# RWKV branch of a hybrid decoder trunk: eight heads in one chain, each head of a pair on its own partition half

## Chip, cores and metric

The kernel runs on one core of a Trainium2 chip. The metric is the device time of one execution in microseconds; a kernel's time is the median of its runs.

## Reference

A trunk of two layers works on 256 tokens of width 1024 in fp32. Each layer adds three branches (RWKV, a short convolution, attention with a forget gate), each behind a sigmoid gate and an up-projection, then `w_out`, a layer norm, a feed-forward part and a second layer norm. The feed-forward part is dense in the first layer, and two of eight experts per token in the second. The change concerns the RWKV branch, with eight heads of 64 channels:

```python
p = p + mu_shift * (token_shift(p) - p)
r, k, v, w_lo, a_lo, g_lo = _split_cols(p, ...)
decay = jnp.exp(-jnp.exp(-jax.nn.softplus(-w_raw) - 0.5))   # w_raw = w0_decay + tanh(w_lo) @ w2_decay
a = jax.nn.sigmoid(a0 + a_lo @ w2_iclr)
g = jax.nn.sigmoid(g_lo) @ w2_gate
kk = _heads(k * k_k); kk = kk / jnp.maximum(jnp.linalg.norm(kk, axis=-1, keepdims=True), 1e-12)
k = k * (1.0 + (a - 1.0) * k_a)
# for each token t and head, a_t = -kk, b_t = kk * a:
state = state * d_t + (state @ a_t) b_t^T + v_t k_t^T ;  y_t = state @ r_t
# then: norm of y per head, times lnx_g plus lnx_b, plus sum(r * k * r_k) * v, times g
```

## The kernel before

The kernel holds activations with channels on partitions and the 256 tokens along the columns, as a tile `[128, j, 256]` for each two heads per 128 channels. The weights of all projections are streamed from HBM on SP's queue in tiles of 1 MB (`st`, three buffers). ScalarE rounds each tile to a high half (`hi`, line 94) and VectorE makes the rest (`lo`, line 97). A product is then three passes of the rounded kind (fp32r): `hi` by `hi`, `hi` by `lo`, `lo` by `hi`. One helper issues them all, and so all carry line 116. The small products of the RWKV branch are ordinary fp32 matmuls with lines of their own.

A scheduler fixes the order of each engine's instructions when the kernel is compiled, and prefers what comes first in the program among what it holds to be ready. So PE's queue in a mixer is a mix: blocks of small RWKV matmuls, and between them runs of projection passes (line 116) of whatever projection comes next.

In a mixer (`mixer_body`) the order of the program is: the projection of the lora inputs (`lo_in`, line 349); the two groups' decay, in-context rate and gate (`lora_group`, line 370, whose matmuls are line 364); then `rwkv_group` twice, for heads 0 to 3 and for heads 4 to 7; then the forget attention (lines 603 to 697), the convolution, the three up-projections. `open_next` (line 700) opens the next stage, and its loads are on SP. What a group does:

- Project k, r and v (`lerp_pair`, line 395: a projection and the token shift), and scale k by its norm. `rs_expand` (line 329) sums squares by head, takes an inverse root, transposes it, and spreads it over the head's channels by a matmul with a constant of four rows (line 344).
- Make `ar` and `bk` (lines 407 to 413), for each chunk of 64 tokens a pair of 64 columns, and from them the score matrix `MT` (line 429), 128 by 128 for each head and chunk: sixteen in a group. A head of a pair has its channels on partitions 0 to 63, the other on 64 to 127.
- Invert the unit triangular 64 by 64 part of each of the sixteen matrices. The diagonal blocks of 16 are inverted by VectorE, a column at a time (lines 447 to 450), all sixteen at once on 64 partitions; then blocks of 32 and of 64 are put together by matmuls, in two halves `q` of eight matrices (lines 472, 477, 481) and one piece of sixteen (line 487). `B` and `BT` (lines 454 to 465) hold the inverse and its transpose.
- Transpose v and `bk` on PE: v by a multiplication with the identity into partitions 64 to 127 (line 498), `bk` by transposes (line 505).
- Run the chain over four chunks (lines 511 to 551). `X` is the state's part (line 515, a state of two heads as a 128 by 128 tile with zeros off the diagonal blocks) plus v's part (line 517); `U` is the inverse by `X` (line 524); the state's update is line 529; the output is the state's part (line 545) plus that of U and v (line 548). ScalarE copies X and U, VectorE updates the state `S`, and GpSimd clears it first (line 532).
- Norm, gain, bonus and gate of y (lines 553 to 567), written to `oh` and `ol` as two halves.

The chain's central lines:

```python
nc.tensor.matmul(pX[:, j, :], ar[:, 4 * j + c, 0, :], Sp[:, j, :], start=True, stop=False)
nc.tensor.matmul(pX[:, j, 64 * h:64 * h + 64], MT[64:128, j, h, c, 0, :], UV[64:128, c, j, h, :], ...)
nc.tensor.matmul(pU[:, j, h, :], TT[:, j, h, c, :], X[:, j, h, :], start=True, stop=True)
nc.tensor.matmul(pD[:, j, :], BKt[:, c, j, :], UV[:, c, j].rearrange("p h v -> p (h v)"), start=True, stop=True)
```

Of the kernel before, what the change touches and what calls it, by code (L numbers as in the profile page):

```python
# [12 lines left out]
F32 = mybir.dt.float32  # L13
F32R = mybir.dt.float32r
# [23 lines left out]
K_ID, K_BO, K_MK, K_M1, K_RST, K_BS, K_EX, K_CM, K_TRI, K_IOTA, NCONST = (  # L38
    0, 128, 256, 384, 448, 704, 706, 962, 1346, 1474, 1602)
# [11 lines left out]
def tile_kernel(ctx, tc, x_in, wmix, wf_in, cols_in, bfor_in, lora_in, lnrow_in, wffn, rw_in, rb_in, wmoe,  # L51
# [202 lines left out]
    LATE = {"cst", "cols", "hcols", "lora", "merged", "raw", "dd", "k", "r", "v", "oh0", "ol0", "oh1", "ol1", "upad", "yv"}  # L254
# [6 lines left out]
    def mixer_body(l, xTh, xTl, mp, lp, es, open_next):  # L261
# [22 lines left out]
        mask1 = cst[0:64, K_M1 - P:K_M1 - 64]  # L284
        bsel = cst[0:64, K_BS - P:K_BS + 2 - P]
        expd = cst[0:4, K_EX - P:K_EX + P]
# [17 lines left out]
        lerp_n = [0]  # L304

        def lerp_pair(key, dst_tag, bufs):
# [6 lines left out]
            o = mt([P, 2, T], dst_tag, bufs=bufs)  # L313
            for j in range(2):
                nc.vector.scalar_tensor_tensor(o[:, j, :], dd[:, j, :], col(C_MU + lerp_n[0]),
                                               raw[:, j, 1:T + 1], ALU.mult, ALU.add)
                lerp_n[0] += 1
            return o

        merged = mt([P, KD, T], "merged")  # L320
# [8 lines left out]
        def rs_expand(sq, scale, eps, op):  # L329
            pc = psC()  # L330
            for tc_ in range(2):
                for j in range(2):
                    nc.tensor.matmul(pc[:, 4 * tc_ + 2 * j:4 * tc_ + 2 * j + 2], sq[:, j, tc_ * P:(tc_ + 1) * P],
                                     bones[:, 0:P:64], start=True, stop=True)
            r8 = sm.tile([P, 8], F32, tag="r8", name=nm("r8"))
            rsqrt_small(r8, pc[:, 0:8], 8, scale, eps, op)
            pt = psC()
            for tc_ in range(2):
                nc.tensor.transpose(pt[0:4, tc_ * P:(tc_ + 1) * P], r8[:, 4 * tc_:4 * tc_ + 4], ident)
# [3 lines left out]
            for j in range(2):  # L343
# [3 lines left out]
        W3 = [P, 2, T]  # L347
        NU = 8
        lo_in = lerp_pair("lo", "lo_in", 1)
# [4 lines left out]
        def lora_mm(g, kind):  # L354
            pz = psC().rearrange("p (j t) -> p j t", j=2)
            for j in range(2):
                ct = 2 * g + j
                if kind == 0:
                    a, b = lora[0:64, ct * P:(ct + 1) * P], lo_in[0:64, 0, :]
                elif kind == 1:  # L360
                    a, b = lora[64:128, ct * P:(ct + 1) * P], lo_in[64:128, 0, :]
                else:
                    a, b = lora[:, 512 + ct * P:512 + (ct + 1) * P], lo_in[:, 1, :]
                nc.tensor.matmul(pz[:, j, :], a, b, start=True, stop=True)
            return pz

        f2 = lambda t: t.rearrange("p j t -> p (j t)")
        u3 = lambda t: t.rearrange("p j (c s) -> p (j c) s", s=64)

        def lora_group(g):  # L370
            sg = mt(W3, "sg")
            tanh2(sg, lora_mm(g, 0), C_W0 + 2 * g)
            half_up(sg)
            cs = mt(W3, "cs")
            for j in range(2):
                nc.vector.tensor_tensor_scan(cs[:, j, :], rst, sg[:, j, :], 0.0, ALU.mult, ALU.add)
            pdec = mt([P, NU, 65], f"pdec{g}")
            nc.gpsimd.memset(pdec[:, :, 0:1], 1.0)
            nc.scalar.activation(pdec[:, :, 1:65], u3(cs), AF.Exp, scale=-DECAY_C)
# [942 lines left out]
```

## Time and profile before

| | us |
|---|---|
| median of 3 runs | 1951.13 |
| lowest and highest run | 1950.76, 1959.35 |
| span of the profiled execution | 1953.1 |
| PE busy in it | 1897.4 |
| VectorE busy | 1529.9 |
| ScalarE busy | 1143.3 |

The profile is one execution, whose span of 1953.1 us stands beside the median of 1951.13. In it the first layer's mixer runs from 16.6 us to some 340, the dense feed-forward part to 553, the second layer's mixer from 570 to some 905, and the experts from 947 to the end. Engines are PE (TensorE), DVE (VectorE), ACT (ScalarE), POOL (GpSimd) and SP; a q behind one is its DMA queue. In rows of PE `a*b` is the stationary operand's shape and `a x b` the result's; `xN` counts passes, of which an ordinary fp32 matmul makes two, and an fp32r matmul or a transpose one. The granted clock is given as a share of 2.4 GHz.

### The profile page before, as it was taken

To read this page: it belongs to the slowest core of one execution; us is meant where nothing else is said; L and a number is where in the kernel's file an instruction comes from. 1 tells how busy PE (TensorE), PEld (TensorE's weight loads), DVE (VectorE), ACT (ScalarE), POOL (GpSimd) and SP (SyncE) were. 2 spreads that over 40 slices of the span, in tenths; PEclk is the share of its full clock that TensorE was granted. 3 is DMA by queue.
4 is the path that set the end of the run, shared out by engine and by line. 5 is a ranking of instruction groups with operands and counts; after the bars stand their busy time and mean duration, and the time that the engine had idled before them with its cause. 6 is when DMAs were issued, how large, how long until landed. Compare 5 with 4: busy or idle time off the path is not lost.

```text
span 1953.1 us, 29168 instructions
## 1 busy us (share of the span) xinstructions
PE 1897.4 (97%) x11285; PEld 1641.8 (84%) x11285; DVE 1529.9 (78%) x2153; ACT 1143.3 (59%) x1460; POOL 40.6 (2%) x94
## 2 busy tenths in 40 slices
PE   7999999999999999999799999999999999999997
PEld 6888899899878888998688888888888888888885
DVE  7958366755569566566899999999899998998987
ACT  5344245344434444344577777777777777777774
POOL 0010000000000010000200000000000000000000
PEclk9999899999999798999799999999999999999998
DMA  7313165555543122486499998999999999899980
GB/s 263 130 46 110 63 216 176 209 180 185 189 166 130 66 87 88 145 328 265 183 377 369 352 370 325 369 370 349 366 333 364 370 355 368 330 356 375 357 314 24
DMA packets 69730, 489.09 MB, mean 250 GB/s; under 512 B 8528, under 2 KB 8784, under 8 KB 11344
## 3 DMA queue, kind: packets, MB, share of 16 engines
q1 hardware_dynamic: 69008, 485.05, 66.9%
q8 instruction: 90, 1.47, 0.3%
q10 hardware_dynamic: 576, 2.10, 0.3%
q14 instruction: 56, 0.46, 0.1%
HBM read 483.98 MB, written 3.15 MB: 249 GB/s over the span
## 4 chain that ended last, share of the span: by engine, by line
PE 59%; DVE 2%; issue 0%; ACT 0%; DVEq 0%
PE A L116 20%; PE B L116 17%; PE C L116 17%; PE Y L977 1%; PE D L977 1%; DVE x L249 0%; PE A L932 0%; PE Y L116 0%; PE D L116 0%; DVE x L242 0%; PE B L932 0%; DVE lo L97 0%; PE Y L1019 0%; PE Y L1018 0%; PE D L1019 0%; PE D L1018 0%
## 5 line engine op out<-in xcount | busy, mean ns | idle before, releaser
L97 DVE TENSOR_TENSOR lo<-st,hi 128x1024 fp32r<-128x1024 f32 x892 | 1050.3, 1220 | 190.8 <-ACT hi L94 156.2
L94 ACT CAST hi<-st 128x1024 fp32r<-128x1024 f32 x896 | 895.8, 1049 | 428.8 <-PE A L116 194.1
L116 PE MATMUL C<-hi,hT 128*128 128x512 f32 x880 | 224.5, 396 | 0.0
L116 PE MATMUL A<-xTh,hi 128*128 128x256 f32 x1280 | 200.8, 296 | 0.0
L116 PEld LDWEIGHTS C<-hi,hT 128*128 128x128 f32 x880 | 164.7, 188 | 37.4 <-ACT hT L979 0.2
L116 PE MATMUL A<-xTl,hi 128*128 128x256 f32 x1280 | 193.3, 290 | 0.0
L116 PE MATMUL A<-xTh,lo 128*128 128x256 f32 x1280 | 191.8, 290 | 0.0
L116 PE MATMUL A<-hi,xTh 128*128 128x512 f32 x448 | 180.7, 403 | 0.0
L116 PEld LDWEIGHTS A<-xTh,hi 128*128 128x128 f32 x1280 | 174.4, 198 | 6.1 <-issue 3.1
L116 PE MATMUL A<-lo,xTh 128*128 128x512 f32 x448 | 175.5, 392 | 0.4 <-DVE lo L97 0.4
L116 PE MATMUL B<-hi,xTh 128*128 128x512 f32 x448 | 175.4, 391 | 0.0
L116 PE MATMUL B<-lo,xTh 128*128 128x512 f32 x448 | 175.1, 391 | 0.0
L116 PE MATMUL A<-hi,xTl 128*128 128x512 f32 x448 | 174.8, 390 | 0.0
L116 PE MATMUL B<-hi,xTl 128*128 128x512 f32 x448 | 174.6, 390 | 0.0
L116 PEld LDWEIGHTS A<-xTl,hi 128*128 128x128 f32 x1280 | 171.3, 196 | 2.9 <-issue 1.1
L116 PEld LDWEIGHTS A<-xTh,lo 128*128 128x128 f32 x1280 | 170.9, 196 | 1.6 <-issue 0.3
L116 PE MATMUL C<-lo,hT 128*128 128x512 f32 x440 | 120.3, 395 | 0.0
L116 PEld LDWEIGHTS A<-lo,xTh 128*128 128x128 f32 x448 | 84.1, 188 | 20.4 <-DVE lo L97 2.4
L116 PEld LDWEIGHTS C<-lo,hT 128*128 128x128 f32 x440 | 83.1, 189 | 19.7
L116 PEld LDWEIGHTS A<-hi,xTl 128*128 128x128 f32 x448 | 84.1, 188 | 18.3
L116 PEld LDWEIGHTS B<-hi,xTl 128*128 128x128 f32 x448 | 84.1, 188 | 18.1
L116 PEld LDWEIGHTS B<-lo,xTh 128*128 128x128 f32 x448 | 84.1, 188 | 17.7 <-issue 0.2
(478 smaller groups left out, 2100.3 us busy)
## 6 DMA issues: line engine op xcount, KB each, us to landing
st<-in_wmoe_dram SPq DMA_DIRECT2D x336, 1024.0 KB, 6.9
st<-in_wmix_dram SPq DMA_DIRECT2D x82, 1024.0 KB, 4.9
st<-in_wffn_dram SPq DMA_DIRECT2D x33, 1024.0 KB, 4.9
xsc<-x ACTq DMA_DIRECT2D x4, 512.0 KB, 4.6
x<-xsc SPq DMA_DIRECT2D x4, 512.0 KB, 5.6
g<-in_lnrow_dram SPq DMA_DIRECT2D x2, 1024.0 KB, 6.5
st<-in_lnrow_dram SPq DMA_DIRECT2D x2, 1024.0 KB, 8.3
cst<-in_const_dram SPq DMA_DIRECT2D x2, 609.0 KB, 11.0
```

Source lines behind the costliest of these rows:

```text
L94: nc.scalar.copy(hi, st[:, h * 1024:(h + 1) * 1024])
L97: (eng or nc.vector).tensor_tensor(lo, st[:, h * 1024:(h + 1) * 1024], hi.bitcast(F32), ALU.subtract)
L116: last = nc.tensor.matmul(o, a, b, start=start and i == 0, stop=stop and i == 2)
L977: nc.tensor.transpose(pt[:, i * P:(i + 1) * P], h[:, i * P:(i + 1) * P], ident)
```

## The change

`rwkv_group` and `lora_group` are gone; their steps stand once, for all eight heads.

- Order: k of both groups, then the norms for all eight heads, then r of both, then v of both. The weight tiles are loaded in the order k0, k1, r0, r1, v0, v1 (before: k0, r0, v0, k1, r1, v1).
- `rs_expand` works on four pairs of heads. The inverse root is split into two halves of the rounded kind in one tile `rT` of 40 rows (rows 0 to 7 and 32 to 39, zeros between), and spread by one fp32r matmul for each pair of heads; its constant `exps` (40 by 512) is a DMA of its own and is cast by ScalarE.
- `bk` holds its two parts in opposite order for the two heads of a pair, so that the head on partitions 0 to 63 and the one on 64 to 127 each have all that belongs to them on their own half. The inverse runs on 128 partitions, both heads of a pair side by side; its matmuls and those of the chain alternate between the two heads, each in its own quarter or half of the array.
- v is transposed by PE transposes ahead of the chain, and its part of X, `XV`, is made ahead of the chain for all chunks; in the chain VectorE adds it to the state's part.
- The state is 64 columns for each pair of heads in place of 128 with zeros, so GpSimd's clears are gone; the last columns of the decay are kept in `PL`. U and the inverse's last copies are shared by ScalarE and VectorE.
- Buffers are shared anew: `MT` takes the place of the lora outputs (`W16`), `UV` of `pdec` and `kx` (`U8`), the transposed `bk` is written in place; the attention's `qk` and `oct_` lie in `merged`'s tile, the first gates' tiles in those of k and r.

```diff
+                for j in range(4):
+                    nc.tensor.matmul(pc[:, 8 * tc_ + 2 * j:8 * tc_ + 2 * j + 2], sq[:, j, tc_ * P:(tc_ + 1) * P],
...
-            rT = mt([4, T], "lo_in")
-            nc.vector.tensor_copy(rT, pt[0:4, 0:T])
-            pe = psC().rearrange("p (j t) -> p j t", j=2)
-            for j in range(2):
-                nc.tensor.matmul(pe[:, j, :], expd[:, j * P:(j + 1) * P], rT, start=True, stop=True)
-            return pe
...
+                nc.tensor.transpose(pt[0:8, tc_ * P:(tc_ + 1) * P], r16[:, 8 * tc_:8 * tc_ + 8], ident)
+            nc.scalar.copy(rT[0:8], pt[0:8, 0:T])
+            nc.vector.tensor_tensor(rT[32:40], pt[0:8, 0:T], rT[0:8].bitcast(F32), ALU.subtract)
...
+            for g in range(2):
+                pe = psC().rearrange("p (j t) -> p j t", j=2)
+                for j in range(2):
+                    nc.tensor.matmul(pe[:, j, :], expdr[:, (2 * g + j) * P:(2 * g + j + 1) * P], rT,
+                                     start=True, stop=True)
+                out.append(pe)
...
+        exps = mt([40, 512], "N1")
+        nc.sync.dma_start(exps, const_in[0:40, NCONST:NCONST + 512])
+        expdr = mt([40, 512], "expdr", F32R)
+        nc.scalar.copy(expdr, exps)
+        rT = mt([40, T], "rT", F32R)
+        nc.vector.memset(rT.bitcast(F32), 0.0)
...
+        k4, r4, v4 = mt(W4, "k"), mt(W4, "r"), mt(W4, "v")
+        for g in range(2):
+            lerp_pair(f"k{g}", k4[:, 2 * g:2 * g + 2], 2 + 6 * g)
...
+        for h in range(2):
+            r = HALF[h]
+            nc.vector.tensor_tensor(bk[r, :, h, :], u4(kx)[r], u4(pinv)[r], ALU.mult)
+            nc.vector.tensor_tensor(bk[r, :, 1 - h, :], u4(k2)[r], u4(pinv)[r], ALU.mult)
...
+        MT = mt([P, 4096], "W16").rearrange("p (h j c a t) -> p h j c a t", h=2, j=4, c=4, a=2)
+        for j in range(4):
+            pS = [psC(), psC()] if j % 2 == 0 else [psD(), psY()]
+            for c in range(4):
+                u = 4 * j + c
+                for h in range(2):
+                    r = HALF[h]
+                    nc.tensor.matmul(pS[h][:, c * P:(c + 1) * P], bk[r, u].rearrange("p a s -> p (a s)"),
+                                     ar[r, u].rearrange("p a s -> p (a s)"), start=True, stop=True)
...
+        dd_ = mt([P, 16, 32], "dblk")
+        for h, hf, r, q in quads:
+            nc.vector.transpose(dd_[r].rearrange("p t s -> p (t s)"),
+                                MTu[h][r, :, 0, q].rearrange("p u (w t) -> p t w u", w=2))
...
+        for t in range(1, 16):
+            nc.vector.tensor_tensor(tmp[:, 0:t, 0:t], tt[:, 0:t, 0:t],
+                                    dg[:, t, 0:t].unsqueeze(1).to_broadcast([P, t, t]), ALU.mult)
+            nc.vector.tensor_reduce(tt[:, 0:t, t], tmp[:, 0:t, 0:t], mybir.AxisListType.X, ALU.add)
...
+        B = mt([P, 16, 64], "B")
+        nc.vector.transpose(flat(B), flat(TT))
...
+        pW = psC().rearrange("p (u s) -> p u s", u=16)
+        for u in range(16):
+            for r in HALF:
+                nc.tensor.matmul(pW[r, u, :].rearrange("p (w r) -> p w r", w=2), N1[r, u, :], Bf[r, u],
+                                 start=True, stop=True)
+        nc.scalar.copy(W1, pW)
+        pX = psC().rearrange("p (u s) -> p u s", u=16)
+        for u in range(16):
+            for r in HALF:
+                nc.tensor.matmul(pX[r, u, :], TT[r, u, :], W1[r, u, :], start=True, stop=True)
+        nc.vector.tensor_tensor(Bf, pX.rearrange("p u (w r) -> p u w r", w=2), Bf, ALU.add)
+        nc.vector.transpose(flat(TT), flat(B))
+        pW = psC().rearrange("p (u s) -> p u s", u=16)
+        up_, dn = [slice(0, 32), slice(64, 96)], [slice(32, 64), slice(96, 128)]
+        for u in range(16):
+            for h in range(2):
+                nc.tensor.matmul(pW[dn[h], u, :], MTu[h][up_[h], u, 0, 32:64], B[up_[h], u, 0:32], start=True, stop=True)
...
+        pX = psC().rearrange("p (u s) -> p u s", u=16)
+        for u in range(16):
+            for h in range(2):
+                nc.tensor.matmul(pX[up_[h], u, :], W2[dn[h], u, :], TT[dn[h], u, 32:64], start=True, stop=True)
...
+        for cc in range(2):
+            pv = psD() if cc else psY()
+            for j in range(4):
+                nc.tensor.transpose(pv[:, j * P:(j + 1) * P], v4[:, j, cc * P:(cc + 1) * P], ident)
...
+        XV = mt([P, 4, 4, 64], "B")
+        for cp in range(2):
+            px = psC().rearrange("p (c j v) -> p c j v", c=2, j=4)
+            for ci in range(2):
+                c = 2 * cp + ci
+                for j in range(4):
+                    for h in range(2):
+                        k_ = HALF[1 - h]
+                        nc.tensor.matmul(px[HALF[h], ci, j, :], MT[k_, h, j, c, 0, :], UV[k_, c, h, j, :],
+                                         start=True, stop=True)
+            nc.scalar.copy(XV[:, 2 * cp:2 * cp + 2], px)
+        for j in range(4):
+            pk = psC()
+            for c in range(4):
+                nc.tensor.transpose(pk[:, c * P:(c + 1) * P], bk[:, 4 * j + c].rearrange("p a s -> p (a s)"), ident)
+            nc.scalar.copy(bk[:, 4 * j:4 * j + 4].rearrange("p c a s -> p c (a s)"), pk.rearrange("p (c n) -> p c n", c=4))
...
+        Sp = None
+        for c in range(4):
+            if c:
+                pX = psC()[:, 0:256].rearrange("p (j v) -> p j v", j=4)
+                for j in range(4):
+                    for r in HALF:
+                        nc.tensor.matmul(pX[r, j, :], ar[r, 4 * j + c, 0, :], Sp[r, j, :], start=True, stop=True)
+                X = mt([P, 4, 64], "dg")
+                nc.vector.tensor_tensor(X, pX, XV[:, c], ALU.add)
+            else:
+                X = XV[:, 0]
+            pU = psC()[:, 0:256].rearrange("p (j v) -> p j v", j=4)
+            for j in range(4):
+                for r in HALF:
+                    nc.tensor.matmul(pU[r, j, :], TT[r, 4 * j + c, :], X[r, j, :], start=True, stop=True)
+            for h, eng in enumerate((nc.scalar.copy, nc.vector.tensor_copy)):
+                eng(UV[HALF[h], c, h], pU[HALF[h]])
+            if c < 3:
+                pD = psD()[:, 0:256].rearrange("p (j v) -> p j v", j=4)
+                for j in range(4):
+                    for h in range(2):
+                        nc.tensor.matmul(pD[HALF[h], j, :], bk[:, 4 * j + c, h, :], UV[:, c, h, j, :],
+                                         start=True, stop=True)
+                Sn = mt([P, 4, 64], "S", bufs=2)
+                pl = PLj[:, :, c:c + 1].to_broadcast([P, 4, 64])
+                if c:
+                    nc.vector.tensor_tensor(Sn, pD, Sp, ALU.add)
+                    nc.vector.tensor_tensor(Sn, Sn, pl, ALU.mult)
+                else:
+                    nc.vector.tensor_tensor(Sn, pD, pl, ALU.mult)
+            py = psY()[:, 0:256].rearrange("p (j t) -> p j t", j=4)
+            if c:
+                for j in range(4):
+                    for r in HALF:
+                        nc.tensor.matmul(py[r, j, :], Sp[r, j, :], ar[r, 4 * j + c, 1, :], start=j == 0, stop=False,
...
+            for j in range(4):
+                for h in range(2):
+                    nc.tensor.matmul(py[HALF[h], j, :], UV[:, c, h, j, :], MT[:, h, j, c, 1, :],
+                                     start=c == 0 and j == 0, stop=True, skip_group_check=True)
+            nc.scalar.copy(y[:, :, 64 * c:64 * c + 64], py)
+            if c < 3:
...
+        oct_ = big[:, 1024:2048].rearrange("p (c n) -> p c n", c=2)
+        gk, gr = mt(W4, "k"), mt(W4, "r")
...
-                qk = mt([72, 2, T], "qk", bufs=2)
+                qk = big[0:72, 512 * h:512 * h + 512].rearrange("p (j t) -> p j t", j=2)
...
```

## Rows read from the trace of the kernel before

**Rows 1.** The page's busy times by engine (its part 1: busy us, share of the span, instructions), and the chain that ended last, its share of the span by engine (part 4).

```profile
PE 1897.4 (97%) x11285; PEld 1641.8 (84%) x11285; DVE 1529.9 (78%) x2153; ACT 1143.3 (59%) x1460; POOL 40.6 (2%) x94
...
PE 59%; DVE 2%; issue 0%; ACT 0%; DVEq 0%
```

**Rows 2.** The view by windows, two stretches of the first layer's mixer: RWKV's whole work, and what follows it up to 345 us. Columns: the window, its length, then busy us (instructions) of PE, PEld, DVE, ACT and POOL, the granted clock of PE as a share of 2.4 GHz, the DMA share and GB/s.

```profile
16.58:258.53 241.95, 236.88 (x1877) 210.97 (x1877) 167.04 (x400) 104.36 (x188) 11.37 (x36) 0.95 0.31 109
258.53:345.00 86.47, 86.47 (x720) 86.20 (x719) 57.66 (x75) 42.96 (x55) 0.44 (x5) 1.00 0.60 209
```

**Rows 3.** The chain of waits in order of time, 800 to 890 us: a run of projections in the second layer's mixer, nothing else between them. Columns: start, length in us, engine, tile, line, instructions.

```profile
821.58 40.31 PE A L116 x336
```

**Rows 4.** The timeline of PE, 218 to 243 us: the chain over chunks in the first layer, with runs of projections between its blocks. Columns: start and length in us, engine, line, operation, out<-in, the sizes, the passes. Lengths overlap at the ends.

```profile
222.23 0.45 PE L548 MATMUL Y<-MT,UV 128*64 128x64 f32 x8
222.62 0.74 PE L116 MATMUL A<-xTl,hi 128*128 128x256 f32 x4
...
230.39 0.43 PE L515 MATMUL D<-S,ar 128*64 128x128 f32 x2
230.75 0.44 PE L517 MATMUL D<-UV,MT 64*64 64x64 f32 x4
231.12 0.43 PE L515 MATMUL D<-S,ar 128*64 128x128 f32 x2
231.49 0.44 PE L517 MATMUL D<-UV,MT 64*64 64x64 f32 x4
231.86 0.74 PE L116 MATMUL A<-xTl,hi 128*128 128x256 f32 x4
232.53 0.67 PE L524 MATMUL D<-X,BT 64*64 64x64 f32 x8
233.13 1.22 PE L116 MATMUL A<-xTh,lo 128*128 128x256 f32 x8
234.19 0.60 PE L529 MATMUL D<-UV,BKt 128*128 128x128 f32 x4
234.72 0.34 PE L548 MATMUL Y<-MT,UV 128*64 128x64 f32 x4
234.99 0.43 PE L545 MATMUL Y<-ar,S 128*128 128x64 f32 x2
235.35 0.34 PE L548 MATMUL Y<-MT,UV 128*64 128x64 f32 x4
235.62 0.73 PE L116 MATMUL B<-oh,hi 128*128 128x256 f32 x4
```

**Rows 5.** The timeline of PE, 24 to 37 us and 60 to 100 us, and last the costliest lines of PE, 0 to 400 us, for line 429 (busy us, mean ns of one | idle time before them and what ended it).

```profile
26.99 1.14 PE L364 MATMUL C<-lo_in,lora 64*128 64x256 f32 x8
28.06 0.39 PE L116 MATMUL A<-xTh,hi 128*128 128x256 f32 x1
...
62.58 1.16 PE L429 MATMUL C<-ar,bk 64*128 64x128 f32 x8
63.66 0.50 PE L116 MATMUL A<-xTl,hi 128*128 128x256 f32 x2
...
L429 PE MATMUL C<-ar,bk 64*128 64x128 f32 x64 | 8.1, 285 | 0.2 <-DVE MT L432 0.2
```

**Rows 6.** The timeline of PE, 100 to 150 us: the solve's matmuls and the transposes of the first group.

```profile
102.98 1.11 PE L472 MATMUL C<-B,N 64*64 64x32 f32 x16
104.03 0.73 PE L116 MATMUL A<-xTl,hi 128*128 128x256 f32 x4
...
108.74 1.19 PE L487 MATMUL C<-BT,dblk 32*32 32x32 f32 x32
109.86 1.09 PE L498 MATMUL C<-ident,v 128*64 128x128 f32 x8
110.88 0.43 PE L681 MATMUL B<-lora,pT 128*128 128x64 f32 x2
...
112.13 0.60 PE L505 MATMUL C<-ident,bk 128*128 128x128 f32 x4
112.66 1.09 PE L498 MATMUL C<-ident,v 128*64 128x128 f32 x8
```

**Rows 7.** The costliest lines of PE, 0 to 400 us, for line 344 (busy us, mean ns of one | idle time before them).

```profile
L344 PE MATMUL C<-lo_in,cst 4*128 4x256 f32 x16 | 4.5, 400 | 0.0
```

**Rows 8.** The waits of PE, 16 to 262 us: the tile and line that waited, who released it, then the total us, the number of waits and the longest.

```profile
PE C L472 <- DVE B L465: 2.4, 2, 1.4
```

**Rows 9.** The view by windows, the four stretches around the solves, two in each layer (columns as in rows 2).

```profile
93.00:114.00 21.00, 20.45 (x209) 18.39 (x210) 8.67 (x25) 9.70 (x22) 1.47 (x4) 0.84 0.29 101
194.00:218.00 24.00, 23.63 (x199) 21.48 (x200) 7.99 (x12) 5.41 (x9) 0.00 (x0) 0.64 0.26 88
646.00:677.00 31.00, 30.76 (x221) 27.85 (x221) 10.35 (x27) 10.20 (x22) 1.47 (x4) 0.56 0.20 68
755.00:769.00 14.00, 13.46 (x104) 12.45 (x104) 6.45 (x9) 2.69 (x6) 0.00 (x0) 0.63 0.28 82
```

**Rows 10.** The view by windows from the first projection to the first solve (columns as in rows 2), and the costliest lines of VectorE in the same stretch, for line 97.

```profile
16.58:93.00 76.42, 73.75 (x517) 66.21 (x516) 68.88 (x138) 37.75 (x53) 4.52 (x19) 1.00 0.46 164
...
L97 DVE TENSOR_TENSOR lo<-st,hi 128x1024 fp32r<-128x1024 f32 x23 | 27.7, 1212 | 0.0
```

**Rows 11.** The timeline of SP's queue: start and length of two issues of DMAs behind the first layer's RWKV work.

```profile
259.66 0.81 SPq L748 DMA_DIRECT2D x<-xsc  x2
```

More of the change, by code (lines that the diff above doesn't have):

```diff
@@ new lines, in mixer_body @@
+        k2 = cs
+        for j in range(4):
+            nc.vector.tensor_scalar(k2[:, j, :], ic[:, j, :], -1.0, col(C_KA + j), ALU.add, ALU.mult)
+        nc.vector.scalar_tensor_tensor(k2, k2, 1.0, k4, ALU.add, ALU.mult)
+        for g in range(2):
+            lerp_pair(f"r{g}", r4[:, 2 * g:2 * g + 2], 4 + 6 * g)
+        ar = mt([P, 16, 2, 64], "ar")
+        bk = mt([P, 16, 2, 64], "bk")
+        nc.vector.scalar_tensor_tensor(ar[:, :, 0, :], u4(kx), -1.0, pdec[:, :, 0:64], ALU.mult, ALU.mult)
@@ new lines, in mixer_body @@
+        for g in range(2):
+            lerp_pair(f"v{g}", v4[:, 2 * g:2 * g + 2], 6 + 6 * g)
+        bon = mt(W4, "bon")
+        for g in range(2):
+            pb = psC().rearrange("p (j t) -> p j t", j=2)
+            nc.tensor.matmul(pb, bones, k2[:, 2 * g:2 * g + 2], start=True, stop=True)
+            nc.vector.tensor_tensor(bon[:, 2 * g:2 * g + 2], v4[:, 2 * g:2 * g + 2], pb, ALU.mult)
+        MT = mt([P, 4096], "W16").rearrange("p (h j c a t) -> p h j c a t", h=2, j=4, c=4, a=2)
[8 more added lines that the diff above has]
+            for h in range(2):
+                nc.vector.tensor_tensor(MT[:, h, j].rearrange("p c a t -> p c (a t)"),
+                                        pS[h].rearrange("p (c n) -> p c n", c=4),
+                                        smask.unsqueeze(1).to_broadcast([P, 4, P]), ALU.mult)
@@ new lines, in mixer_body @@
+        for w in range(2):
+            nc.vector.tensor_scalar(dd_[:, :, 16 * w:16 * w + 16], tt.rearrange("p c s -> p s c"),
+                                    bsel[:, w:w + 1], None, ALU.mult)
+        TT = mt([P, 16, 64], "BT")
+        flat = lambda t: t.rearrange("p u s -> p (u s)")
+        nc.gpsimd.memset(TT, 0.0)
+        for h, hf, r, q in quads:
+            nc.vector.transpose(TT[r, :, q].rearrange("p u (w t) -> p t w u", w=2), flat(dd_[r]))
+        B = mt([P, 16, 64], "B")
+        nc.vector.transpose(flat(B), flat(TT))
@@ new lines, in mixer_body @@
+        for g in range(2):
+            pm = psC().rearrange("p (j t) -> p j t", j=2)
+            nc.tensor.matmul(pm, bones, y[:, 2 * g:2 * g + 2], start=True, stop=True)
+            nc.vector.scalar_tensor_tensor(y[:, 2 * g:2 * g + 2], pm, -1.0 / 64, y[:, 2 * g:2 * g + 2],
+                                           ALU.mult, ALU.add)
+        sq = mt(W4, "BT")
+        nc.scalar.activation(sq, y, AF.Square)
+        for g, pe in enumerate(rs_expand(sq, 1.0 / 64, RWKV_EPS, ALU.add)):
+            for j in range(2):
+                ct = 2 * g + j
+                yj = y[:, ct, :]
+                nc.vector.scalar_tensor_tensor(yj, yj, col(C_LG + ct), pe[:, j, :], ALU.mult, ALU.mult)
+                nc.vector.scalar_tensor_tensor(yj, yj, col(C_LB + ct), bon[:, ct, :], ALU.add, ALU.add)
```

330 lines of the change are left out of this document (100 added, 230 removed).

## Prediction

> **What bounds the kernel now.** I read the page's busy times and its chain first [rows 1]: TensorE is busy for 97% of the span, and the chain that ended last runs over it for 59% of the span, with no other engine above 2%. A chain on PE alone can still hide waits, so the two mixers were read next, by stretch [rows 2]. In the first mixer the RWKV work lasts from the first projection at 16.58 us to the last write of `ol` at 258.53 us; behind it come 86.5 us in which PE does nothing but projections at full clock. In the RWKV stretch PE is just as busy, yet it moves only 1877 instructions in 242 us, against 720 of the long ones in 86.5 us, and the granted clock is 0.95. So RWKV's end is not what the mixer waits for: 86 us of other work stand behind it. What counts is how much of PE's time RWKV takes from the projections that fill the gaps, and what it does to the clock. The price of a projection pass (line 116, 256 columns) is 40.31 us for 336, 0.120 us each [rows 3]. Everything behind the mixers (dense FFN, experts) is untouched.
>
> **The change part by part.** All times below are start to start: a block's price is the start of the next row less its own. An ordinary fp32 matmul is two passes on PE in these rows, a transpose one.
>
> The chain over four chunks. Now it runs twice a layer. One chunk of one group [rows 4] costs 0.36 + 0.37 + 0.37 + 0.37 (lines 515 and 517 in turns), 0.60 (524), 0.53 (529) and 0.27 + 0.36 + 0.27 (548, 545, 548), together 3.50 us. The first chunk has no state: 0.60 (517, eight passes at 524's price) + 0.60 + 0.53 + 0.39 = 2.12 us, the last no state update: 2.97. That is 2.12 + 2 x 3.50 + 2.97 = 12.1 a group, 24.2 a layer. Afterwards there are 17 blocks of 16 passes (three for the state's part of X, four for U, three for the update, seven for the output), each head of a pair in its own half of the array. What such passes cost is the main choice. Line 548 alternates between the two column halves: 4 passes 0.27 us, 8 passes 0.39 [rows 4], so 0.03 us a pass more. Line 517 and line 524 stay in one corner: 4 passes 0.37, 8 passes 0.60, so 0.058. I take 0.03 for all pairs, because the same gain is seen for two row halves: line 364 in turns takes 1.07 us for 8 passes of 256 columns, line 429, which stays in one half, 1.08 us for 8 of only 128 [rows 5]. A block of 16 is then 0.39 + 8 x 0.03 = 0.63, and 17 are 10.7: saves 13.5 us a layer. At 0.058 for the ten blocks of 64 rows (1.06 each) it saves 9.2.
>
> The triangular solve's matmuls. Now, per layer, four pieces each of lines 472, 477 and 481 and two of line 487. Line 472 costs 1.05 for 16 passes, 477 has the same shape; line 487 costs 1.12 for 32 passes, 0.035 each, and 481 is taken at that [rows 6]: 4.2 + 4.2 + 2.2 + 2.2 = 12.9. Afterwards four blocks of 64: two at 0.39 + 56 x 0.03 = 2.07, two of 32 rows at 64 x 0.035 = 2.24, together 8.6: saves 4.3 (0.8 if pairs don't overlap).
>
> Transposing v. Now line 498 multiplies by the identity, 1.02 us for 8, 4.1 a layer; afterwards eight transposes, priced as line 505 at 0.53 for 4 [rows 6], 1.06: saves 3.0. X's part of v leaves the chain (its passes are counted there now) for two blocks of 32, 0.39 + 24 x 0.03 = 1.11 each: costs 2.2 (4.0 without overlap).
>
> The score products (line 429), 8.1 us busy a layer [rows 5]: in turns between the row halves 16 passes should take the 1.07 us of line 364's eight double-length ones, 4.3 in all: saves 3.8 (or nothing). The expansion of the norms (line 344, 4.5 us a layer [rows 7]) becomes eight single fp32r passes of 256 columns in two places. The nearest row is the projection's 0.12; with 0.15 for each entry that is 1.3: saves 3.2. If they cost what line 344 costs a pass, half of 4.5 is left: saves 2.2.
>
> Sum: 13.5 + 4.3 + 3.0 - 2.2 + 3.8 + 3.2 = 25.6 us a layer, 51.2 for two; without any overlap 11.2 and 22.4.
>
> Entries. A run of projection passes between RWKV blocks costs more than its passes: 0.67 for 4 (0.48 dense) and 1.06 for 8 (0.96) [rows 4], some 0.15 a run. A chunk shows three runs; one chain in place of two saves 12, the solve in four blocks and not fourteen pieces 10, half of the norm steps 6: 28 runs a layer, 4.2 us, 8.4 in all. This is also where something speaks against the change: lines 515 and 517, in turns, pay 0.37 for 4 passes where 4 more in one block cost 0.23. The Trainium skill (TensorEngine Tiling (Array Packing), Key Properties) says that a change of the tiling mode drains the engine, and the trace agrees with that 0.14. If the scheduler cuts each of the 17 new blocks once for a run of projections, 17 x (0.15 + 0.14) = 4.9 a layer eat this gain.
>
> Waits and clock. PE waits 2.4 us in the first layer for B from VectorE, in two waits [rows 8], one for each group's solve; one is left, 2.4 saved in two layers. Behind every such wait the granted clock falls from 2.4 to 1.2 GHz for a time: the four stretches have 0.84 of 21 us, 0.64 of 24, 0.56 of 31 and 0.63 of 14 [rows 9], so 3.4 + 8.6 + 13.6 + 5.2 = 30.8 us of PE's time are lost. Two of the four solves remain: 15.4 saved, between nothing (the remaining stretches grow to double) and 30.8.
>
> What costs nothing, and under which cover. VectorE's and ScalarE's steps on all eight heads have the same number of columns or half the instructions, since partitions 64 to 127 were idle in the solve; VectorE is 68.9 us busy of the 76.4 before the first solve's end, 27.7 of it the weights' `lo` [rows 10], so it is nearly full there and hidden only as long as projections are ready. The queues: one more DMA of 80 KB on SP, behind that of `bfor` and in front of the third weight tile; two issues there take 0.81 us [rows 11], so 0.4 each, bound 0 to 0.5 a layer. ScalarE's cast of it waits for the landing, and casts of later weights stand behind it; their tiles are 1 MB each and land after it on the same queue, so they wait for their tile and not for this cast. GpSimd loses six clears of the state a layer and is 2% busy. Weight tiles come in the order k, k, r, r, v, v, same sizes and same queue. `open_next` puts its loads on SP behind the last RWKV tile that is freed (at 259.66 us); RWKV now ends sooner, so they stand in nobody's way.
>
> All in all 51.2 + 8.4 + 2.4 + 15.4 = 77.4 us. The profiled execution spans 1953.1 us, 2.0 more than the median of 1951.1, so 1953.1 - 77.4 - 2.0 = 1874 us.
>
> **The rivals.** (a) Pairs don't overlap: two heads in opposite corners take turns as if in one. For it: no row shows opposite corners, only halves side by side or one above the other. Against: 0.03 us in line 548. Then 22.4 + 8.4 + 2.4 + 15.4 = 48.6 are saved: 1902 us. The Trainium skill (TensorE: Matmul & The Clock Gate, section "Wait — 56ns, not 53.3ns?") also names a floor of some 62 ns per matmul where the sequencer's program decodes it; an estimate by it would be 592 passes x (62 - 30) ns = 18.9 a layer less than my sum, 1912 us. Lines 548 and 487 at 30 and 35 ns speak against it.
>
> (b) The clock stays up after the one solve, since its blocks are denser and fewer: 30.8 in place of 15.4, 1858 us. Against: the wait for B is still there.
>
> (c) Slower: the one solve starves PE. B for all eight heads now needs VectorE's whole work before any solve matmul may run. VectorE's part that isn't `lo` is 68.9 - 27.7 = 41 us for the first group; some 25 us of the second group's come on top, and if they push `lo` back, PE runs out of projections for 25 us a layer and then stays at the lower clock to the chain's end, 60 us or so, 30 lost. 1953.1 - 59.6 - 30.8 + 2 x 55 - 2.0 = 1971 us. It decides from a loss of 45 us a layer on. Against: now too the solve is interleaved with `lo`, and PE shows 1.2 us of wait for it.
>
> (d) The RWKV work is hidden anyway, and its end isn't what matters, so nothing moves: 1951. PE has no room in which it could be hidden [rows 2], so this is little.
>
> **How the numbers follow.** Forecast 0.58, (a) 0.17, (b) 0.14, (c) 0.07, (d) 0.04. The range 1845 to 1910 takes in (a) and (b), both ends of the clock, and the block that is cut; it leaves out (c), (d) and the floor of 62 ns. A measurement of this kernel tells 0.5% from no change: faster by more 0.89, within 0.04, slower 0.07.
>
> **What would show it.** In the profile after: blocks of 16 near 0.63 us in the chain (1.06: rival a); 17 of them a layer; one stretch of lowered clock a layer, not two; one wait for B a layer near 1.2 us (over 10: rival c); RWKV's last write well before 200 us in the first layer, then projections alone at 0.120; spans behind the mixers as now. I am wrong in the mechanism if the mixers shorten and the blocks don't.

## The result and the profile after

The changed kernel takes 1894.28 us (median of 4 runs, 1893.41 to 1895.49) against 1952.95 us: a ratio of 0.9692, 95% interval 0.9671 to 0.9714. The forecast was 1874 with a range of 1845 to 1910. Its profiled execution spans 1892.8 us, 60.3 less than before; 77.4 were forecast. One number needs a remark: executions of one and the same kernel differ here by up to 18 us, and their mean granted clock with them (the kernel before gave 1947.4 us at 0.978 and 1965.2 at 0.967, the first experiment 1885.1 at 0.979 and 1898.3 at 0.971), so differences of some us between experiments are read at a like clock.

The page's busy times and the chain that ended last, after ([rows 1] before):

```profile
PE 1825.1 (96%) x11357; PEld 1592.5 (84%) x11357; DVE 1492.4 (79%) x1949; ACT 1136.8 (60%) x1440; POOL 33.6 (2%) x74
...
PE 90%; DVE 7%; ACT 1%; issue 1%; DMA 1%; SPq 0%; ACTq 0%; DVEq 0%
```

PE is busy for 72.3 us less, and the span is only 60.3 shorter: PE is idle for 1892.8 - 1825.1 = 67.7 us, 12.0 more than before (1953.1 - 1897.4 = 55.7). VectorE now stands in the chain with 7%. Its 2% before is no match for that: 59% and 2% are all that chain holds, since it could be followed back only to 755.5 us, so it said nothing of the first mixer, in the prediction too. The two stretches of the first mixer by windows (columns as in rows 2): RWKV's last write of `ol` now starts at 176.7 us, not at 258.9.

```profile
16.00:175.00 159.00, 149.03 (x1455) 132.53 (x1454) 119.34 (x253) 71.61 (x129) 5.88 (x20) 0.91 0.30 107
175.00:320.00 145.00, 144.90 (x1190) 143.24 (x1189) 88.71 (x122) 72.95 (x107) 0.43 (x5) 1.00 0.56 195
```

The chain on PE's timeline, one chunk ([rows 4] before). Each block has 16 passes; start to start they take 0.62, 0.52, 0.56, 0.52 and 0.56 us, for all eight heads:

```profile
143.15 0.68 PE L548 MATMUL C<-dg,BT 64*64 64x64 f32 x16
143.77 0.44 PE L702 MATMUL B<-ident,s 128*128 128x128 f32 x2
...
144.79 0.69 PE L555 MATMUL D<-U,bk 128*64 128x64 f32 x16
145.31 0.64 PE L572 MATMUL Y<-W,U 128*64 128x64 f32 x16
145.87 0.43 PE L705 MATMUL B<-lora,pT 128*128 128x64 f32 x2
...
146.97 0.68 PE L540 MATMUL C<-S,ar 64*64 64x64 f32 x16
147.49 0.63 PE L568 MATMUL Y<-ar,S 64*64 64x64 f32 x16
148.05 0.33 PE L702 MATMUL B<-ident,s 128*128 128x128 f32 x1
```

Where the waiting is: PE's timeline around the solve (the bracket is idle time and who ended it), and VectorE's queue in the same time.

```profile
82.33 0.39 PE L108 MATMUL A<-hi,xTh 128*128 128x512 f32 x1
89.26 0.79 PE L108 MATMUL A<-hi,xTh 128*128 128x512 f32 x1 [6.55 <-DVE yv L638]
...
111.98 2.51 PE L482 MATMUL C<-B,N 64*64 64x32 f32 x64 [1.94 <-DVE B L472]
...
116.00 3.63 PE L488 MATMUL C<-N,BT 64*64 64x32 f32 x64
```

```profile
78.69 4.33 DVE L451 STREAM_TRANSPOSE dblk<-W 32x512 f32<-32x512 f32 x4
83.05 1.22 DVE L476 TENSOR_TENSOR N<-W,cst 64x1024 f32<-64x1024 f32 x1
...
88.73 0.47 DVE L638 TENSOR_SCALAR yv<-A,bfor 8x256 f32<-8x256 f32 x1
```

Line 638 is the addition of the attention's forget bias, half a microsecond. It frees one of the two PSUM banks of pool A, and stands in VectorE's queue behind the large solve's transposes and masks. PE's next projection needs that bank, and all that is queued behind it on PE waits too: 6.5 us here, 7.8 in the second layer. Before, the same wait was 0.5 us in the first layer and 0.4 in the second:

```profile
PE A L108 <- DVE yv L615: 0.5, 1, 0.5
```

The clock in the stretches around the two solves ([rows 9] before):

```profile
88.00:95.00 7.00, 5.49 (x17) 4.09 (x17) 6.73 (x24) 4.71 (x7) 0.10 (x1) 0.65 0.26 74
114.00:135.00 21.00, 21.00 (x307) 18.94 (x305) 5.72 (x16) 7.92 (x17) 0.73 (x2) 0.53 0.15 52
615.00:640.00 25.00, 22.69 (x121) 19.26 (x121) 23.55 (x54) 12.26 (x18) 1.57 (x5) 0.86 0.49 168
640.00:675.00 35.00, 33.90 (x529) 30.29 (x529) 14.09 (x41) 14.04 (x33) 2.21 (x6) 0.71 0.19 63
```

These lose 2.5 + 9.9 + 3.5 + 10.2 = 26.0 us, where before 30.8 were lost. There are two solves in place of four, but around each of them 12.3 and 13.7 us are lost, where before it was 7.7 in the mean.

### The profile page after: what moved, and what is told of

Read it like the earlier page. It is cut to its first block, busy times and chain, and to the rows that moved or that the text cites. A ratio compares the mean times of both kernels' runs of the same rounds, so it can differ in the third digit from the quotient of the medians.

```text
span 1892.8 us, 29012 instructions
## 1 busy us (share of the span) xinstructions
PE 1825.1 (96%) x11357; PEld 1592.5 (84%) x11357; DVE 1492.4 (79%) x1949; ACT 1136.8 (60%) x1440; POOL 33.6 (2%) x74
## 4 chain that ended last, share of the span: by engine, by line
PE 90%; DVE 7%; ACT 1%; issue 1%; DMA 1%; SPq 0%; ACTq 0%; DVEq 0%
PE A L116 38%; PE B L116 20%; PE C L116 19%; PE D L116 1%; PE Y L116 1%; DVE lo L97 1%; PE Y L1001 1%; PE D L1001 1%; PE B L686 1%; ACT hi L94 0%; DVE BT L470 0%; DVE dblk L451 0%; PE B L702 0%; DVE x L249 0%; PE C L488 0%
## 5 line engine op out<-in xcount | busy, mean ns | idle before, releaser
L116 PE MATMUL A<-xTh,hi 128*128 128x256 f32 x1280 | 192.3, 290 | 0.0
L116 PE MATMUL A<-xTl,hi 128*128 128x256 f32 x1280 | 188.9, 288 | 0.0
L116 PE MATMUL A<-xTh,lo 128*128 128x256 f32 x1280 | 186.2, 286 | 0.2 <-DVE lo L97 0.2
L116 PEld LDWEIGHTS A<-xTh,hi 128*128 128x128 f32 x1280 | 170.3, 195 | 2.4 <-ACT lora L666 0.8
```

Source lines behind the costliest of these rows:

```text
L116: last = nc.tensor.matmul(o, a, b, start=start and i == 0, stop=stop and i == 2)
```

## Experiments

My theory: the blocks got as short as forecast, and what is missing is PE's waiting for VectorE's queue and the lowered clock behind it. The rivals: PE is short of work in any case; the order made at compile time is at fault; the pairs' overlap is not what made the blocks short. In the table idle is the span less PE's busy time in the profiled execution, and the clock is its mean granted share of 2.4 GHz. Each ratio is against the kernel before as it ran beside that experiment; its median was 1953.0 to 1959.5 us, so small differences are better read from the ratios than from the medians.

| run | median us | ratio, 95% interval | idle us | clock |
|---|---|---|---|---|
| the change | 1894.3 | 0.9692 (0.9671 to 0.9714) | 67.7 | 0.973 |
| e1_pf_bank | 1885.5 | 0.9652 (0.9615 to 0.9690) | 65.8 | 0.979 |
| e2_unpaired | 1924.4 | 0.9832 (0.9807 to 0.9856) | 67.1 | 0.968 |
| e3_noloop | 1900.6 | 0.9703 (0.9675 to 0.9730) | 72.8 | 0.971 |
| e4_oldnorm | 1882.0 | 0.9620 (0.9597 to 0.9644) | 63.7 | 0.982 |
| e5_fv_pool | 1901.3 | 0.9723 (0.9684 to 0.9762) | 67.1 | 0.972 |
| e6_scores | 1892.0 | 0.9682 (0.9640 to 0.9725) | 69.6 | 0.978 |
| e7_dve_more | 1911.1 | 0.9771 (0.9732 to 0.9810) | 88.7 | 0.968 |
| e8_comb | 1897.4 | 0.9699 (0.9669 to 0.9729) | 64.5 | 0.972 |
| e9_act_more | 1873.2 | 0.9566 (0.9525 to 0.9608) | 60.5 | 0.980 |
| e10_hi_as_lo | 1866.3 | 0.9535 (0.9496 to 0.9573) | 58.7 | 0.987 |
| e11_fv_early | 1880.4 | 0.9595 (0.9549 to 0.9640) | 61.3 | 0.980 |
| e12_both | 1885.7 | 0.9601 (0.9569 to 0.9634) | 58.2 | 0.974 |

**Do pairs overlap?**

```diff
-            for j in range(4):
-                for r in HALF:
+            for r in HALF:
+                for j in range(4):
                     nc.tensor.matmul(pU[r, j, :], TT[r, 4 * j + c, :], X[r, j, :], start=True, stop=True)
```

The same turn was made in the other nine blocks' loops.

> The changed kernel with the loops of each small block turned round in the solve, in v's part of X and in the chain: all matmuls of the head on partitions 0 to 63 first, then all of the other, same instructions. Theory 1 (two heads in opposite corners of the array run at the same time only when they are neighbours in PE's queue): a block of 16 passes costs up to 1.06 in place of 0.55 us; 10 chain blocks of 64 rows, the solve and XV together some 10 us a layer more, about 1914 us, up to 1923. Theory 2 (a pass costs 0.03 us anyway, in any order): 1892 to 1896 us.

1924.4 us, 30 more than the change with equal idle time; some 10 of the 30 are the mean clock (1922.2 x 0.032 = 61.5 us lost, against 1892.8 x 0.027 = 51.1). The costliest lines of PE up to 345 us (busy us, mean ns of one), first the run, then the change up to 330 us:

```profile
L523 PE MATMUL C<-U,W 64*64 64x64 f32 x64 | 6.6, 314 | 0.0
...
L548 PE MATMUL C<-dg,BT 64*64 64x64 f32 x48 | 2.9, 224 | 0.0
```

```profile
L523 PE MATMUL C<-U,W 64*64 64x64 f32 x64 | 3.5, 289 | 0.0
...
L548 PE MATMUL C<-dg,BT 64*64 64x64 f32 x48 | 2.0, 224 | 0.0
```

The same instructions in another order cost half as much again (548), or nearly twice as much (523, part of it at the lower clock). Theory 1 holds: here heads in opposite corners overlap only as neighbours in PE's queue. That decides rival (a): it was wrong here.

**Scores.** The score products came out at some 6.4 us from start to start in the first layer (6.3 busy), not 4.3.

```diff
-            pb = psC().rearrange("p (j t) -> p j t", j=2)
+            pb = psB().rearrange("p (j t) -> p j t", j=2)
```

> The changed kernel with the bonus product in pool B and no longer in pool C, so that the two banks of the first score products are free together and the two heads of a pair stand in turns in PE's queue. Theory 1 (two heads run at the same time only as neighbours): line 440 falls from 6.4 and 7.2 us to about 4.3 a layer. What it does to the time: PE waits for VectorE a little later, so the 5 us turn up as waiting, 1892 to 1896 us. Theory 2 (the scores' time is paid in full): 1889 us. Theory 3 (pairs of 128 columns don't overlap): line 440 stays.

PE's timeline, one block of 16 of the scores: in the change, 1.55 us (72.62 to 74.17), and in the run, 1.00 us:

```profile
72.62 1.71 PE L440 MATMUL C<-ar,bk 64*128 64x128 f32 x16
74.17 0.38 PE L440 MATMUL D<-ar,bk 64*128 64x128 f32 x2
```

```profile
69.58 1.16 PE L440 MATMUL C<-ar,bk 64*128 64x128 f32 x16
70.58 0.27 PE L440 MATMUL D<-ar,bk 64*128 64x128 f32 x1
```

In the change one of the two banks was not yet free, so the scheduler put the first head's products ahead of the second's. Mending that shortened the first blocks, and the later ones waited for VectorE's masks. All of line 440 fell from 6.3 to 5.3 us of PE's busy time in the first layer and from 7.3 to 5.9 in the second, not to 4.3. The time is that of the change within its interval.

**Is it the bank?**

```diff
-        pf = psA()[0:8, 0:T]
+        pf = psB()[0:8, 0:T]
```

> The changed kernel with one edit: the small forget projection pf is accumulated in a bank of pool B and no longer in one of pool A, so the next projections of pool A do not need VectorE's read of it. Theory 1 (the missing gain is PE waiting for that read, which stands in VectorE's queue behind the one large solve): the waits of 6.5 and 7.8 us are gone, with 2 us of lowered clock behind each, so about 1894 - 14 - 4 = 1876 us. Theory 2 (VectorE sets the end of the solve, and PE has no other work): PE waits the same time later, at line 482 for B; 1892 to 1896 us.

The waits of PE, first and second layer:

```profile
PE A L109 <- DVE lo L97: 4.8, 1, 4.8
...
PE A L109 <- DVE lo L97: 7.5, 1, 7.5
```

The wait only moved, a little further down PE's queue, to the next thing that VectorE's queue holds back. Of the 9 us only 1.9 are idle time; the rest goes with the clock (0.979), and one of the four executions, at 0.971, took 1898.3 us, so even the 9 us are not sure. Theory 1 falls as to the bank; VectorE's queue stays.

**Does VectorE set it?** More work, with the same result:

```diff
+            for _ in range(4):
+                nc.vector.tensor_tensor(N1[r], MTu[h][r, :, 0, :], mask1[r]...to_broadcast([64, 16, 64]), ALU.mult)
```

> The changed kernel with the masking of N1 done five times over with the same result: eight more VectorE instructions of 1.2 us in the solve, 9.2 us a layer. Theory 1 (VectorE sets when the solve can begin, and PE's other work has run out): PE waits 9 us more a layer, 1894 + 18 = 1912 us, more if the clock falls for longer. Theory 2 (the projections cover it): 1892 to 1896 us.

1911.1 us. PE's waits grow by 10.0 and 10.7 us for 9.2 us more on VectorE a layer:

```profile
PE A L108 <- DVE yv L640: 16.5, 1, 16.5
...
PE A L108 <- DVE yv L640: 18.5, 1, 18.5
```

Less work, by leaving it out in two places:

> The changed kernel without the 30 VectorE instructions of the column loop: the diagonal blocks of 16 are taken as identities, so the inverse is not the reference's. B is ready some 9 us earlier. Theory 1 (the wait for B makes the clock fall for some 20 us at half speed, 10 us lost a layer): the wait of 2 us and what is lost behind it vanish, 1894 - 4 - 20 = 1870 us. Theory 2 (the clock falls from the short passes themselves, whatever the wait): only the waits are gone, 1890 us. Theory 3 (PE is idle for VectorE's sake elsewhere): also the waits for the forget projection shrink, below 1870 us.

```diff
-        for t in range(1, 16):
-            nc.vector.tensor_tensor(tmp[:, 0:t, 0:t], ...)
-            nc.vector.tensor_reduce(tt[:, 0:t, t], ...)
```

All three theories of it were wrong: 1900.6 us, and idle for 5 us more. The waits for the forget projection, 14.3 us in the change, are gone, but those for B grow from 4.1 to 22.8. The scheduler moved line 482 (478 here) up to where it now thought B to be ready, ahead of the projections that had filled the time, and PE stood still for 10.4 and 12.4 us. A gain on VectorE that the order on PE has already spent brings nothing.

```profile
93.20 3.63 PE L478 MATMUL C<-B,N 64*64 64x32 f32 x64 [10.43 <-DVE B L468]
```

> The changed kernel with the high halves of the r and v weights used in place of the low ones too, so that eight of VectorE's 1.2 us instructions a layer, all ahead of the scores, are left out (the low parts of these weights are missing from the result and the high ones are counted twice); PE's passes are the same. Theory 1 (VectorE is full there, and its work ahead of the solve sets PE's waits): VectorE has 9.8 us less a layer, the waits of 8 to 10 us a layer vanish: some 1876 us, less with a higher clock. Theory 2 (the order made at compile time): it moves the solve forward by as much and the waits stay, 1890 us or more.

```diff
+            if key[0] in "rv":
+                ...
+                los = his
```

This removes work ahead of the scores and not inside the solve, and here theory 1 holds: 1866.3 us. The waits at line 108 fall from 6.5 and 7.8 us to 3.1 and 3.2, no wait for B is left, and the clock stays at 1.00 all through both solves. So what VectorE has to do ahead of the solve sets these waits, though not one for one: of the 26.8 us by which the span is shorter, 9.0 are idle time of PE and 17.8 its shorter busy time at the higher clock. This run is the fastest, and it computes less.

**Where could VectorE's work go?** To GpSimd, the low halves of two weight tiles (in this run and in all that follow but e4_oldnorm, the forget projection is in pool B, as above):

```diff
-            his, los = weight(f"fv{s}")
+            his, los = split(ahead.pop(f"fv{s}", None) or load(wmix[l, MIX[f"fv{s}"]]), eng=nc.gpsimd)
```

> The changed kernel with the forget projection in pool B as in the run before, and GpSimd in place of VectorE making the low halves of the two weight tiles behind it (four instructions a layer). Theory 1 (VectorE's queue is what PE waits for between the scores and the solve): the waits at lines 108 and 109 go, VectorE has 4.8 us less to do ahead of B a layer, so PE's idle time falls by some 10 us in two layers: about 1875 us against 1885 of the run with the bank alone. Theory 2 (PE is short of work there in any case, or GpSimd is too slow for the low halves): PE waits for GpSimd or for B instead, 1885 us or more.

1901.3 us, slower than the bank alone. One VectorE instruction, the same in both kernels, in the change and then in the run, with GpSimd's instruction that ran beside it (65.4 us is the first start):

```profile
L416 DVE SCALAR_TENSOR_TENSOR ar<-U x2: 1219/1219/1219, 62.0 to 589.7; 128x1024 f32<-128x1024 f32 x2
```

```profile
L416 DVE SCALAR_TENSOR_TENSOR ar<-U x2: 3384/3404/3423, 65.4 to 600.5; 128x1024 f32<-128x1024 f32 x2
...
64.79 6.20 POOL L97 TENSOR_TENSOR lo<-st,hi 128x1024 fp32r<-128x1024 f32 x2 [0.43 <-ACT hi L94]
```

It took 2.2 us longer, more than the 1.2 us instruction that VectorE had been relieved of. In the first layer each of GpSimd's four instructions stretches one of VectorE's in this way, and VectorE's busy time is 5.4 us more than with the bank alone (1498.1 against 1492.7), with eight instructions fewer. In e8_comb (below) the same instruction, with nothing on GpSimd beside it, took 1.22 us, and another of only 16 columns, 0.17 us elsewhere, took 2.33 and ended when GpSimd's did:

```profile
57.62 2.33 DVE L133 SCALAR_TENSOR_TENSOR r<-nr_t,nr_r 128x16 f32<-128x16 f32 x1
...
57.34 2.58 POOL L97 TENSOR_TENSOR lo<-st,hi 128x1024 fp32r<-128x1024 f32 x1 [4.70 <-ACT hi L94]
```

To ScalarE, three small things:

```diff
-                    (nc.scalar.copy if h else nc.vector.tensor_copy)(UV[...], pv[...])
+                    nc.scalar.copy(UV[...], pv[...])
...
-        nc.vector.tensor_scalar(fb, pf, bfor, None, ALU.add)
+        nc.scalar.activation(fb, pf, AF.Identity, bias=bfor)
...
-            nc.vector.tensor_scalar(dd_[...], tt.rearrange("p c s -> p s c"), bsel[:, w:w + 1], None, ALU.mult)
+            nc.scalar.activation(dd_[...], tt.rearrange("p c s -> p s c"), AF.Copy, scale=bsel[:, w:w + 1])
```

> The changed kernel with the forget projection in pool B, and ScalarE in place of VectorE for the copies of v's transposes, the addition of the forget bias and the scaling of the inverted blocks: some 3 us less on VectorE a layer around the solve, same PE work. Theory 1 (VectorE's work between the scores and the solve sets PE's waits one for one): idle time of PE falls by 6 us against the run with the bank alone, 1879 us at the same granted clock. Theory 2 (PE waits because the order made at compile time calls for results too early, whatever VectorE has to do): the waits stay at their 14 us, 1885 us or more.

```profile
PE A L109 <- DVE lo L97: 2.1, 1, 2.1
...
PE A L109 <- DVE lo L97: 4.9, 1, 4.9
```

2.7 and 2.6 us less of waiting than with the bank alone, for some 3 us taken from VectorE: nearly one for one, theory 1. PE's idle time falls by 5.3 us, where 6 were expected, and at nearly the same clock the time falls by 6.1 (1879.7 us at 0.980, against 1885.8 at 0.979), some 2 of it for that 0.001. It is the fastest kernel that computes all of it: 1873.2 us.

Or earlier, in the program's order:

```diff
+        fvw = [weight(f"fv{s}") for s in range(2)]
         MT = mt([P, 4096], "W16")...
...
-            his, los = weight(f"fv{s}")
+            his, los = fvw[s]
```

> The changed kernel with the forget projection in pool B and the halves of the two weight tiles behind it made ahead of the scores in the program, so that their low halves stand ahead of the solve in VectorE's queue. Nothing is added or left out. Theory 1 (VectorE is full, and what PE gains at line 109 it waits for B): the idle time stays near 14 us, 1883 to 1894 us with the clock. Theory 2 (only the order on VectorE is at fault): PE has 11 us of work while VectorE transposes, the wait at line 109 goes, 1876 us.

1880.4 us. The wait at line 109 is gone, and some of it is now a wait of 4.1 us in the first and 3.7 us in the second layer for ScalarE's copy of that product: between the theories.

**The clock.** The ordinary norm expansion:

```diff
-                    nc.tensor.matmul(pe[:, j, :], expdr[:, ...], rT, start=True, stop=True)
+                    nc.tensor.matmul(pe[:, j, :], exps[0:8, ...], rT, start=True, stop=True)
```

> The changed kernel with the norms' expansion as ordinary fp32 matmuls of 8 rows (two passes each of 256 columns) in place of one fp32r pass with a split of two halves. Theory 1 (PE is the bound there, each of the passes counts): line 342 goes from 1.3 to about 4 us a layer, 1894 + 5 = 1899 us. Theory 2 (this stands before the solve, where VectorE is the bound, so PE's time there is free): 1893 to 1896 us.

Both were wrong: it is 12 us faster than the change, with line 342 (341 here) at 3.8 us and not 1.3. PE arrives at the waits later and idles 4.0 us less, so the expansion's saving was no time at all; the rest is the clock, which stays at 1.00 through both solves. The run also leaves out ScalarE's cast and copy for the split (1132.9 us busy, not 1136.8); what they do to the waits was not tested apart.

> Both banks' edits, GpSimd's low halves and the ordinary norm expansion together. Theory 1 (VectorE's queue, then the clock): the waits shrink as in the run with GpSimd and the clock stays up as in the run with the ordinary expansion: 1870 us. Theory 2 (the gain of the ordinary expansion was its delay of PE alone, and it is paid once PE doesn't wait): 5 us over the run with GpSimd.

That gain isn't one that adds up: e8_comb joins the edits of e1_pf_bank, e6_scores, e5_fv_pool and e4_oldnorm, and takes 1897.4 us at 0.972, 4 less than e5_fv_pool; both theories missed it.

> The edits of the run with ScalarE's share and of the run with the early forget weights together: 3 us less on VectorE a layer, and the two low halves ahead of the solve. Theory 1 (VectorE's queue sets PE's waits): the remaining waits of 2.1 and 4.9 us at line 109 go and at most half of them comes back as a wait for B or for the attention's tiles; 1866 to 1870 us at the same granted clock. Theory 2 (the idle time is fixed by the plan): 1873 us or more.

e12_both joins the edits of e9_act_more and e11_fv_early. It has the least idle time of all (58.2 us), and yet 1885.7 us. Windows of the first layer's solve and the row of its first matmul, first in e9_act_more, then in e12_both:

```profile
110.00:131.00 21.00, 19.54 (x405) 17.97 (x405) 13.22 (x31) 10.56 (x25) 1.48 (x4) 1.00 0.16 52
...
114.99 2.06 PE L482 MATMUL C<-B,N 64*64 64x32 f32 x64 [1.46 <-DVE B L472]
```

```profile
120.00:141.00 21.00, 21.00 (x333) 18.92 (x331) 7.50 (x18) 6.89 (x18) 0.74 (x2) 0.54 0.15 52
...
119.17 2.06 PE L483 MATMUL C<-B,N 64*64 64x32 f32 x64 [1.35 <-DVE B L473]
```

A wait of 1.46 us leaves the clock up, one of 1.35 us comes before some 19 us at half of it. These are two programs; e6_scores shows the same within one, with the same matmuls of the solve in its first and its second layer (the row of the first matmul, then the window):

```profile
112.11 2.93 PE L482 MATMUL C<-B,N 64*64 64x32 f32 x64 [1.99 <-DVE B L472]
...
112.00:134.00 22.00, 21.89 (x345) 19.91 (x347) 7.85 (x21) 7.50 (x16) 0.74 (x2) 0.53 0.14 49
```

```profile
642.55 2.06 PE L482 MATMUL C<-B,N 64*64 64x32 f32 x64 [2.08 <-DVE B L472]
...
645.00:667.00 22.00, 22.00 (x443) 19.20 (x443) 9.59 (x31) 13.58 (x33) 1.64 (x5) 1.00 0.17 59
```

So neither the length of the wait for B nor the small matmuls behind it decide alone, and neither theory of the run saw this.

## Why the prediction was right, and where it was off

- The chain's blocks: forecast 0.63 us for 16 passes, 10.7 a layer; measured 0.52 to 0.62, mean 0.56, so 9.5. Taking 0.03 us a pass for opposite corners, from rows that showed only halves, held, on the condition of neighbours. Of the floor for one matmul in the Trainium skill (TensorE: Matmul & The Clock Gate, section "Wait — 56ns, not 53.3ns?"), taken for each pass as my estimate took it, these blocks show no sign: 0.56 for 16 is 0.035 us a pass. For a whole matmul of two passes that is 0.070 us, above the floor, so they can't tell whether it holds there.
- The solve's matmuls: forecast 8.6 us a layer. They take 9.9 in the change, much of it at half clock, and 6.4 at full clock (the run with the ordinary expansion). v's part of X: forecast 2.2, 3.35 in the change, 2.2 at full clock.
- The score products: forecast 4.3, measured 6.3 and 7.3, for want of neighbours in part: with them in the first blocks, e6_scores still has 5.3 and 5.9. The norms' expansion: forecast 1.3, measured 1.3, and worth no time, since PE waits behind it.
- Entries: 8.4 were forecast. The projections' three groups of pool A, 1280 passes each before and after, are 18.5 us less busy, first before, then after; how much of it is the clock was not separated. Counted in the traces, the two mixers' 161 unbroken runs of line 116 became 90: 71 fewer, where 56 were forecast, so by the forecast's 0.15 us a run the term is 10.7.

```profile
L116 PE MATMUL A<-xTh,hi 128*128 128x256 f32 x1280 | 200.8, 296 | 0.0
...
L116 PE MATMUL A<-xTl,hi 128*128 128x256 f32 x1280 | 193.3, 290 | 0.0
L116 PE MATMUL A<-xTh,lo 128*128 128x256 f32 x1280 | 191.8, 290 | 0.0
```

```profile
L116 PE MATMUL A<-xTh,hi 128*128 128x256 f32 x1280 | 192.3, 290 | 0.0
L116 PE MATMUL A<-xTl,hi 128*128 128x256 f32 x1280 | 188.9, 288 | 0.0
L116 PE MATMUL A<-xTh,lo 128*128 128x256 f32 x1280 | 186.2, 286 | 0.2 <-DVE lo L97 0.2
```

- Waits: this step failed. I counted one wait for B in place of two, 2.4 us saved. There is one a layer, as counted, but of 1.9 and 2.1 us in place of 1.2, and PE's idle time grew by 12.0. The sentence at fault is the one on cover: VectorE "is nearly full there and hidden only as long as projections are ready". They were not. From 60 us to the solve's first matmul (93 us before, which the prediction called the solve's end, and 112 after), VectorE is full in both, but for 52 us in place of 33, and PE is idle for 9.3 us of them in place of 1.5:

```profile
60.00:93.00 33.00, 31.51 (x211) 26.92 (x209) 31.68 (x71) 12.67 (x15) 1.71 (x6) 1.00 0.28 102
...
60.00:112.00 52.00, 42.71 (x291) 35.77 (x290) 50.71 (x93) 17.36 (x25) 1.61 (x5) 0.93 0.28 96
```

The eight heads' steps came ahead of the first solve, and the second group's projections no longer covered them: line 116 fills 13.3 of the 33 us before, and 0.2 of the 32.5 after, from 67 us, just ahead of the scores, to 99.5 us. That is the mechanism of rival (c), with 14.3 us of waiting in two layers (0.9 before) and not its 45 a layer, and not at B but at a bank whose reader stood in the same queue. More work on VectorE made these waits longer (e7_dve_more), less made them shorter (e9_act_more, e10_hi_as_lo); another bank or another order only moves them (e1_pf_bank), makes them longer (e3_noloop) or takes a part away (e11_fv_early).
- Clock: 15.4 were forecast and 4.8 came (26.0 lost in place of 30.8). Half as many solves does not mean half the lost time. The sign of one lowered stretch a layer did not come: there are two, one behind the wait for the bank and one behind that for B. And "behind every such wait" held for the four waits before, but not for those of 1.46 us in e9_act_more and 2.08 in e6_scores.
- The sum: of the 17.1 us that are missing, waits account for 12.0 + 2.4 = 14.4 and the clock for 10.6; that leaves 7.9 the other way, by subtraction, for the blocks and entries. Of it the fewer runs explain 2.3; the rest was not measured term by term.

The range held because it allowed for a clock that saves nothing ("the remaining stretches grow to double"), and because a part of the waits was made up by the blocks and entries. That was luck in part: the range left (c) out, and (c) came, only smaller. Nor does the time alone speak for the mechanism, since 1894 stands nearer to the 1902 of rival (a) than to 1874; the blocks' rows and e2_unpaired do.

Still open: what decides whether the clock falls at a solve, and for how long, and so why kernels with equal work differ by 10 us.

## To carry to other kernels

When several small problems are merged into one, its serial preparation on another engine comes in one piece, and the work that covered it is gone: sum that engine's queue up to the merged step, and look for small instructions in it that free a buffer which the bottleneck needs. Two matmuls in different corners of the array overlapped here only as neighbours in the queue, so give both their PSUM banks at the same time. A saving on an engine that waits right behind it is no saving.

## What was not expected of the hardware

VectorE's instruction of 1.22 us took 3.4 us while GpSimd ran a tensor instruction of its own beside it, so work given to GpSimd can cost VectorE as much as it takes. Four executions of one program took 1885.1 to 1898.3 us, with a mean granted clock of 0.979 to 0.971. The same solve behind a wait of 2 us ran at a granted clock of 0.53 in one layer and at 1.00 in the other.
